# Splitting w_o beside the last group of products, and putting a chunk's state and the next chunk's turning side by side in a Mamba-2 and pooling step

## The chip, the cores and the metric

The kernel runs on one core of a Trainium2 chip. A core has a matrix engine (TensorE, "PE" in the profile, with its weight loads as "PEld"), a vector engine (VectorE, "DVE"), a scalar engine (ScalarE, "ACT"), a general engine (GpSimd, "POOL") and a queue engine (SyncE, "SP") that only issues DMAs. The metric is the device time of one execution in microseconds (us), as the median of several runs. Line numbers (L1213 and so on) are those of the kernel before.

## The reference, cut to what matters

One layer is computed for 1024 prompt positions and 64 sample positions (T = 1088 in all) with a model width of 1024:

```python
proj = h @ w_in                                   # u_pool, z_pool, z_ssm, xBC, dt, g
p = (pool_mix(u_pool) * silu(z_pool)) @ w_pool_out
# SSD over chunks of 128 positions, 4 groups of 8 heads, for every chunk in turn:
acs   = cumsum(dq * A);  decay = exp(acs_i - acs_j) under the causal mask
att   = (Cq Bq^T) * decay * dq
y     = att @ xq + (Cq * exp(acs)) @ h            # within the chunk, and from the state
h     = h * exp(last) + Bq^T ((exp(last - acs) * dq) * xq)
y     = rmsnorm((y + D * x) * silu(z_ssm)) ;  s = y @ w_ssm_out
x     = x + gate * ((sigmoid(g_pool) * p + sigmoid(g_ssm) * s) @ w_o)
```

All is float32. The large products are done as three passes of a shorter format (fp32r): a matrix is split into a high part (a rounded copy) and a low part (the difference), and hi·hi, hi·lo and lo·hi are added up in PSUM. A split therefore takes one copy on ACT and one subtraction on POOL or DVE.

## The kernel before

**Stages.** Up to 818 us of the profiled execution the kernel normalises the input, makes the projection with `w_in` and handles the sample positions. Then comes the **chunk stage**, which the change reorders: 32 chunks of the prompt (4 groups of heads, `g`, times 8 chunks of 128 positions, `c`), run one after the other. The change calls one of these a row of the sequence, and the prediction does so too. Beside the rows run the **products**: 8 units of `w_pool_out` (P_unit, L1711) and 24 units of `w_ssm_out` for the first three groups (S_unit, L1727), each in three pieces of 12 matmuls (L359 to L361), 96 pieces in all. After them comes the **last group of products**, S_unit for group 3 with the merging of the branches (tail_unit, L1907), and then the **output rows**, the product with `w_o` (from L1978).

**A row** is the generator `chunk` (L1488), cut by `yield` into steps that the loop at L1798 calls by hand:

1. loads (L1490 to L1494) of x, B and C (`xb`) and of the decay exponents (`dec`), 3 buffers each;
2. exponentials: ACT makes `cE` (L1498), POOL masks `dec` (L1192), ACT takes 8 exponentials (L1201);
3. **turning** (L1502 to L1525): PE transposes x and B (L1506, L1508) and multiplies B with C (L1509) into the PSUM tiles `px` and `pbc`; ACT copies `bt` (L1511) and C into `pbc` (L1513); DVE makes `xd` (L1517), `xw` (L1519), `dec` times CB (L1520) and `cE` times C (L1522); ACT makes `xD` (L1525);
4. **state and sums** (L1527 to L1543): PE makes the update `pu` (L1530, needs `bt` and `xw`) and the 16 products of `inner` (L1213 with `xd` and `dec`, L1216 with the state and `cE`); POOL scales the state (L1536), DVE adds `pu` (L1538); DVE adds the sums (`v`, L1542) and `finish` gates and squares them (L1468 to L1479);
5. for the last chunk of a group, the final state is turned and stored (L1546 to L1551).

**What sets the order.** All matmuls that are traced between two calls of `in_line` (L1792 and L1822) are chained, so PE does them exactly as the loop traces them. On ACT, DVE, POOL and SP a scheduler orders instructions by trace order among those that its own timeline has ready; each engine then works strictly in that order. `products(t)` (L1785) makes pieces until 2.56 times `t` have been made, so a row gets two or three. `behind(engine, n)` queues the instructions of a block behind the n-th last one traced on that engine; rows 1 and 2 are turned behind DVE (L1802). PSUM has three buffers for products (PA), four for px, pbc and the sums (PB) and one for `pu` (PC). Before the loop, 4 pieces (FRONT) are made and row 0 is turned.

**w_o before.** `wo_splits` (L1766) reads `w_o` in 16 halves of 256 KB (`pw`, two buffers), copies the high part on ACT (`ph`, L1777, one buffer), stores it from ACT's queue (L1778), subtracts on POOL (L1779) and stores the low part from SP (L1773), all to DRAM (`wo_d`). It is called from the thirteenth row of the loop on. In the last group of products, `wo_prep(k)` (L1859) loads both parts back. `m_split` (L1868) splits the merged branch, and `samples[m]` multiplies its sample positions (L1877).

Of the kernel before, what the change touches and what calls it, by code (L numbers as in the profile page):

```python
# [8 lines left out]
F32 = mybir.dt.float32  # L9
F32R = mybir.dt.float32r  # L10
AF = mybir.ActivationFunctionType
ALU = mybir.AluOpType
# [8 lines left out]
P = 128  # L21
D = 1024
# [24 lines left out]
def tile_pool_ssd_step(  # L47
# [6 lines left out]
    nc = tc.nc  # L54
    uid = [0]

    def nm(s):
        uid[0] += 1
        return f"{s}_{uid[0]}"
# [10 lines left out]
    def open_(name, bufs, side="left"):  # L70
        cm = tc.tile_pool(name=name, bufs=bufs, side=side, reuse_waits="tile")
        kept.append(cm)
        return cm.__enter__()
# [36 lines left out]
    load = nc.sync.dma_start  # L110
    store_ = nc.scalar.dma_start
    mm = nc.tensor.matmul
    act = nc.scalar.activation
    V = nc.vector
# [275 lines left out]
    def dram(name, shape, dt=F32):  # L390
        return dr.tile(list(shape), dt, tag=name, name=name)
# [13 lines left out]
    def behind(engine, n=0):  # L405

        of = (i for i in reversed(nc.cur_bb.bb.instructions) if i.engine == engine)
        for _ in range(n):
            next(of)
        return tc.issue_after(next(of))  # L410
# [1280 lines left out]
    seq = []  # L1691
# [14 lines left out]
    ck = right.__enter__()  # L1706
# [48 lines left out]
    def pieces():  # L1755
        ws = first_ws
        nxt = len(ws)
        for i, (pf, run) in enumerate(prods):
            while nxt < len(prods) and nxt <= i + 1:
                ws[nxt] = prods[nxt][0]()  # L1760
                nxt += 1
            yield from run(ws.pop(i))
    pc_ = pieces()
    wo_d = [dram(f"wo{k}", [P, 2, D]) for k in range(8)]

    def wo_splits():  # L1766
        raws = {}
        for n in range(18):
            if n < 16:
                raws[n] = ck.tile([P, 512], F32, tag="pw", name=nm("pw"), bufs=2)  # L1770
                load(raws[n], w_o[0, n // 2 * P:n // 2 * P + P, n % 2 * 512:n % 2 * 512 + 512])
            if n > 1:
                load(wo_d[(n - 2) // 2][:, 1, n % 2 * 512:n % 2 * 512 + 512], raws.pop(n - 2))  # L1773
            yield
            if n < 16:
                hi = ck.tile([P, 512], F32R, tag="ph", name=nm("ph"), bufs=1)
                act(hi, raws[n], AF.Copy)  # L1777
                store_(wo_d[n // 2][:, 0, n % 2 * 512:n % 2 * 512 + 512], hi.bitcast(F32))  # L1778
                nc.gpsimd.tensor_tensor(raws[n].bitcast(F32R), raws[n], hi.bitcast(F32), ALU.subtract)  # L1779
            yield  # L1780
    wos = wo_splits()
    RATE = 2.56
    FRONT = 4

    def products(t):  # L1785

        nonlocal made
        while made < RATE * t:
            next(pc_, None)
            made += 1  # L1790
# [5 lines left out]
        next(pc_)  # L1796
    next(seq[0])
    for i in range(len(seq)):  # L1798
        if i > 12:
            next(wos, None)  # L1800
        if i + 1 < len(seq):
            with behind(mybir.EngineType.DVE, 1 - i) if i < 2 else ExitStack():  # L1802
                next(seq[i + 1])
        products(i + 0.4)
        if i > 0:
            next(seq[i - 1], None)
        if i > 12:
            next(wos, None)
        next(seq[i], None)
        if i % NC == 3:  # L1810
            sample_end(i // NC)
        if i + 3 < len(seq):
            next(seq[i + 3])
        if i + 2 < len(seq):
            with behind(mybir.EngineType.Activation) if i == 0 else ExitStack():
                next(seq[i + 2])
        products(i + 1.0)
    next(seq[-1], None)
    for it in (pc_, wos):
        for _ in it:  # L1820
            pass
    in_line((mybir.EngineType.PE,))  # L1822
    right.__exit__(None, None, None)
    while right_all:
# [3 lines left out]

    mp = ctx.enter_context(tc.tile_pool(name="mp", bufs=8, side="right", reuse_waits="tile"))
    mq = open_("mq", 5)  # L1830

    def M(shape=(P, T), dt=F32):
        return mq.tile(list(shape), dt, tag="m", name=nm("m"))
# [7 lines left out]
    for c in range(9):  # L1841
        n = min(P, T - c * P)
# [5 lines left out]
    for c in range(9):  # L1848
        n = min(P, T - c * P)
# [4 lines left out]
    wo, mh, ml = [None] * 8, [None] * 8, [None] * 8  # L1854
    w4 = [Y4(hp), Y4(hp)]
    pso = [PB(), PC()]
    samples = []

    def wo_prep(k, mem):  # L1859
        if k < 4:  # L1860
            hi, lo = w4[0][:, k, :D], w4[1][:, k, :D]
        else:
            hi, lo = mem((P, D), F32R), mem((P, D), F32R)
        load(hi.bitcast(F32), wo_d[k][:, 0])
        load(lo.bitcast(F32), wo_d[k][:, 1])
        wo[k] = (hi, lo)

    def m_split(k, mem):  # L1868

# [37 lines left out]
    def tail_unit(m):  # L1907
        pf, run_ = S_unit(3, m, m_done)

        def run(w):  # L1910
            for _ in run_(w):
                pass
            if m < 5:
                wo_prep(m, M)
            if m < 7:
                m_split(m, M8 if m < 4 else G)
            if m < 5:
                with tc.high_priority(PRIO):
                    samples[m]()
        return (pf, run)  # L1920
    run_units([tail_unit(m) for m in range(8)])
    y4 = [Y4(hs), Y4(hs)]
# [4 lines left out]
    for k in (5, 6):  # L1927
        wo_prep(k, late)
        samples[k]()
# [119 lines left out]
```

## Time and profile before

| | us |
|---|---|
| median of 3 runs (1295.9 to 1298.21) | 1296.04 |
| the profiled execution, its own time | 1297.28 |
| its span, first to last instruction | 1295.4 |
| up to the first product beside the rows | 818.5 |
| opening, to the first product after row 0 | 18.8 |
| rows 1 to 31 with their products | 275.7 |
| rest of the products, last group of products | 83.8 |
| output rows, end | 98.6 |

The mean granted clock of TensorE is 0.996. In the profile's timeline a row gives start, duration, engine, line, operation, output and inputs, count, and in brackets how long the engine sat idle before it and what ended that. Matmuls overlap: the distance from one start to the next is the time one takes, and the duration (0.32 us for a distance of 0.16) is longer. A row "x4" merges four neighbours.

### The profile page before, as it was taken

The numbers are of one execution on the slowest core, as the hardware profiler recorded it, in microseconds if no ns is written. First come the engines' busy times: TensorE is split into PE (matmuls) and PEld (weight loads), VectorE is DVE, ScalarE is ACT, GpSimd is POOL, SyncE is SP. The second block draws the span as 40 slices with busy tenths as digits, with TensorE's granted clock in tenths as the row PEclk, the third lists the DMA queues.
The fourth block names the chain that finished last, engine by engine and source line by source line (L and its number), as shares of the span: only waits on it lengthen the run. The fifth ranks groups of instructions, "written<-read, shape, count | busy, mean of one in ns | idle before, by whom it ended". The sixth has DMA issues, their size and how long they took to land.

```text
span 1295.4 us, 26382 instructions
## 1 busy us (share of the span) xinstructions
PE 1258.9 (97%) x9739; PEld 1170.7 (90%) x9739; DVE 893.3 (69%) x1512; ACT 699.5 (54%) x1658; POOL 671.9 (52%) x563
## 2 busy tenths in 40 slices
PE   7999999999999999999999999999998999999998
PEld 6779999989999999999999999888897889999786
DVE  4686678966979688676766675577665877476433
ACT  4665347365656555555666543687886776201111
POOL 1007668677868777564445444266675656214000
PEclk9999999999999999999999999999999999999999
DMA  9736355465456544444566574999887665475631
GB/s 330 242 115 223 113 163 164 147 203 177 136 161 212 157 144 149 151 146 135 169 182 192 154 207 159 336 362 382 296 270 249 200 210 171 160 262 161 227 105 50
DMA packets 233793, 251.68 MB, mean 194 GB/s; under 512 B 31265, under 2 KB 177905, under 8 KB 233658
## 3 DMA queue, kind: packets, MB, share of 16 engines
q1 hardware_dynamic: 161568, 171.60, 41.6%
q10 hardware_dynamic: 72098, 78.41, 17.6%
q8 instruction: 77, 1.26, 0.4%
q14 instruction: 50, 0.41, 0.1%
HBM read 167.06 MB, written 83.01 MB: 193 GB/s over the span
## 4 chain that ended last, share of the span: by engine, by line
PE 73%; issue 8%; DMA 6%; POOL 4%; ACT 4%; DVE 4%; ACTq 0%; SPq 0%; POOLq 0%; DVEq 0%
PE mm L608 7%; PE ps L608 7%; PE ps L609 7%; PE ps L610 7%; PE mm L610 6%; PE mm L609 6%; PE mm L359 4%; PE mm L360 4%; PE mm L361 4%; PE ps L1213 2%; PE ps L1997 2%; PE ps L1995 2%; PE ps L1996 2%; PE pc L1530 2%; PE ps L1216 2%
## 5 line engine op out<-in xcount | busy, mean ns | idle before, releaser
L168 POOL TENSOR_TENSOR wlo<-rawA,whi 128x512 fp32r<-128x512 f32 x120 | 180.0, 1505 | 176.8 <-ACT whi L165 100.3
L168 POOL TENSOR_TENSOR wlo<-raw,whi 128x512 fp32r<-128x512 f32 x92 | 147.2, 1607 | 123.2 <-ACT whi L165 109.3
L359 PE MATMUL mm<-Y,whi 128*128 128x352 f32 (+1 forms) x480 | 164.2, 342 | 2.0 <-ACT G L1739 1.4
L360 PE MATMUL mm<-Y,whi 128*128 128x352 f32 (+1 forms) x480 | 158.1, 329 | 1.0 <-DVE Y L1566 1.0
L361 PE MATMUL mm<-Y,wlo 128*128 128x352 f32 (+1 forms) x480 | 157.5, 328 | 0.0
L608 PE MATMUL mm<-Y,whi 128*128 128x272 f32 x496 | 146.5, 295 | 0.7 <-DVE GA L624 0.5
L610 PE MATMUL mm<-Y,wlo 128*128 128x272 f32 x496 | 144.2, 291 | 2.9 <-POOL wlo L168 2.4
L608 PE MATMUL ps<-Y,whi 128*128 128x272 f32 x496 | 143.4, 289 | 2.3 <-ACT o L808 2.2
L609 PE MATMUL ps<-Y,whi 128*128 128x272 f32 x496 | 143.0, 288 | 0.0
L609 PE MATMUL mm<-Y,whi 128*128 128x272 f32 x496 | 142.6, 288 | 0.0
L610 PE MATMUL ps<-Y,wlo 128*128 128x272 f32 x496 | 142.6, 287 | 0.0
L1056 DVE SCALAR_TENSOR_TENSOR GA<-GA,cvT,GA 128x1112 f32<-128x1112 f32 x72 | 128.5, 1787 | 1.6 <-ACT GA L1053 1.5
L165 ACT ACTIVATE whi<-rawA 128x512 fp32r<-128x512 f32 x125 | 78.3, 627 | 88.8 <-PE ps L609 44.9
L165 ACT ACTIVATE whi<-raw 128x512 fp32r<-128x512 f32 x96 | 58.9, 627 | 105.7 <-DVE raw L554 51.3
L359 PEld LDWEIGHTS mm<-Y,whi 128*128 128x128 f32 x480 | 90.8, 189 | 8.8 <-issue 4.6
L610 PEld LDWEIGHTS mm<-Y,wlo 128*128 128x128 f32 x496 | 93.4, 188 | 4.7 <-POOL wlo L168 3.5
L608 PEld LDWEIGHTS mm<-Y,whi 128*128 128x128 f32 x496 | 93.3, 188 | 3.4 <-ACT whi L165 0.7
L608 PEld LDWEIGHTS ps<-Y,whi 128*128 128x128 f32 x496 | 93.3, 188 | 2.9 <-ACT o L808 2.4
L609 PEld LDWEIGHTS mm<-Y,whi 128*128 128x128 f32 x496 | 93.4, 188 | 0.9
L610 PEld LDWEIGHTS ps<-Y,wlo 128*128 128x128 f32 x496 | 93.4, 188 | 0.0
L609 PEld LDWEIGHTS ps<-Y,whi 128*128 128x128 f32 x496 | 93.3, 188 | 0.0
L360 PEld LDWEIGHTS mm<-Y,whi 128*128 128x128 f32 x480 | 90.8, 189 | 1.7 <-DVE Y L1566 1.6
(450 smaller groups left out, 3801.1 us busy)
## 6 DMA issues: line engine op xcount, KB each, us to landing
rawA<-in_w_in SPq DMA_DIRECT2D x46, 512.0 KB
dec<-acs_d SPq DMA_DIRECT2D x32, 512.0 KB
xbc<-GA ACTq DMA_DIRECT2D x24, 512.0 KB
xb<-xbc SPq DMA_DIRECT2D x32, 384.0 KB
rawA<-in_w_in SPq DMA_DIRECT2D x32, 256.0 KB
pw<-in_w_ssm_out ACTq DMA_DIRECT2D x32, 256.0 KB
ws<-ph ACTq DMA_DIRECT2D x32, 256.0 KB
ws<-pw SPq DMA_DIRECT2D x32, 256.0 KB
```

Source lines behind the costliest of these rows:

```text
L165: ins = act(hi[:, :, :ncols], raw[:, :, :ncols], AF.Copy)
L168: (eng or nc.gpsimd).tensor_tensor(lo[:, :, :ncols], raw[:, :, :ncols], hi[:, :, :ncols].bitcast(F32), ALU.subtract)
L359: mm(ps[:, :n], a, rh[k][:, o:o + n], start=(k == 0), stop=False)
L360: mm(ps[:, :n], a, rl[k][:, o:o + n], start=False, stop=False)
L361: mm(ps[:, :n], b, rh[k][:, o:o + n], start=False, stop=(k == nk - 1))
L608: mm(p, hi, ah, start=(k == 0), stop=False)
L609: mm(p, hi, al, start=False, stop=False)
L610: mm(p, lo, ah, start=False, stop=(k == 3))
L1056: V.scalar_tensor_tensor(d[:, :n], rp[:, k:k + n], cvT[:, 24 * k + mc:24 * k + mc + 1], d[:, :n], ALU.mult, ALU.add)
L1213: mm(o[hh], xd[:S, 2 * q + hh, :], dec[:S, 2 * q + hh], start=True, stop=state is None)
L1216: mm(o[hh], state[:, h * 64:h * 64 + 64], cE[:, h], start=False, stop=True)
L1530: mm(pu, bt, xw.rearrange("p h d -> p (h d)"), start=True, stop=True)
```

## The change

In the loop, the products between a row's turning and the next state go, and the order is turned round: row i's state and sums come first, right behind them row i+1 is turned, and then all the products of the row follow in one block. `wo_splits` goes from the loop. Instead `wo_prep` splits the first five slices of `w_o` (k < LATE = 5) in SBUF beside the last group of products, from raw slices of 512 KB; for the last three, `wo_store` splits them there too (low part on DVE), stores them in DRAM from SP, and `wo_prep` loads them back as before. `samples[m]` is called one unit later. A new pool `mr` holds two raw slices and one high part.

```diff
@@ the loop over the rows (-1796, +1781) @@
-        if i > 12:
-            next(wos, None)
+        if i > 0:
+            next(seq[i - 1], None)
+        next(seq[i], None)
         if i + 1 < len(seq):
             with behind(mybir.EngineType.DVE, 1 - i) if i < 2 else ExitStack():
                 next(seq[i + 1])
-        products(i + 0.4)
-        if i > 0:
-            next(seq[i - 1], None)
-        if i > 12:
-            next(wos, None)
-        next(seq[i], None)
         if i % NC == 3:
             sample_end(i // NC)
...
         products(i + 1.0)
@@ wo_prep (-1861, +1841) @@
-        load(hi.bitcast(F32), wo_d[k][:, 0])
-        load(lo.bitcast(F32), wo_d[k][:, 1])
+        if k < LATE:
+            raw = mr.tile([P, D], F32, tag="wr", name=nm("wr"))
+            load(raw, w_o[0, k * P:k * P + P, :])
+            act(hi, raw, AF.Copy)
+            nc.gpsimd.tensor_tensor(lo, raw, hi.bitcast(F32), ALU.subtract)
+        else:
+            load(hi.bitcast(F32), wo_d[k][:, 0])
+            load(lo.bitcast(F32), wo_d[k][:, 1])
...
+    def wo_store(k):
+        raw = mr.tile([P, D], F32, tag="wr", name=nm("wr"))
+        load(raw, w_o[0, k * P:k * P + P, :])
+        hi = mr.tile([P, D], F32R, tag="wh", name=nm("wh"), bufs=1)
+        act(hi, raw, AF.Copy)
+        load(wo_d[k][:, 0], hi.bitcast(F32))
+        V.tensor_tensor(raw.bitcast(F32R), raw, hi.bitcast(F32), ALU.subtract)
+        load(wo_d[k][:, 1], raw)
@@ tail_unit (-1910, +1905) @@
-            if m < 5:
+            if m < LATE:
                 wo_prep(m, M)
             if m < 7:
                 m_split(m, M8 if m < 4 else G)
-            if m < 5:
+            if 1 < m < 5:
+                wo_store(m + 3)
+            if 0 < m <= LATE:
                 with tc.high_priority(PRIO):
-                    samples[m]()
+                    samples[m - 1]()
```

More of the change, by code (lines that the diff above doesn't have):

```diff
@@ L1763, in tile_pool_ssd_step @@
     pc_ = pieces()
[L1764 to L1781, printed above, removed]
+    LATE = 5
+    wo_d = {k: dram(f"wo{k}", [P, 2, D]) for k in range(LATE, 8)}
     RATE = 2.56
@@ L1818, in tile_pool_ssd_step @@
     next(seq[-1], None)
-    for it in (pc_, wos):
-        for _ in it:
-            pass
+    for _ in pc_:
+        pass
     in_line((mybir.EngineType.PE,))
@@ L1830, in tile_pool_ssd_step @@
     mq = open_("mq", 5)
+    mr = open_("mr", 2)
     def M(shape=(P, T), dt=F32):
```

## The prediction, made before the change was run

> **What bounds the kernel now.** I read the page's busy shares first, then the engines' busy time by stage.
>
> ```profile
> PE 1258.9 (97%) x9739; PEld 1170.7 (90%) x9739; DVE 893.3 (69%) x1512; ACT 699.5 (54%) x1658; POOL 671.9 (52%) x563
> ```
> ```profile
> 837.30:1113.00 275.70, 270.51 (x2179) 240.03 (x2178) 198.77 (x269) 202.68 (x562) 177.96 (x205) 1.00 0.79 259
> 1113.00:1196.80 83.80, 83.21 (x492) 80.78 (x493) 50.51 (x89) 10.63 (x18) 23.92 (x13) 0.98 0.63 218
> ```
>
> PE is the bound in both stages the change touches: it is idle 5.2 of 275.7 us in the rows, 0.6 of 83.8 us in the last group. The change takes no matmul away. So it can win only seams between matmuls of different kinds and the little idle time, and it can lose wherever PE now has to wait. The second step was therefore PE's timeline, start by start, around one row (from 910 us), and at the first and last row with sums from the state.
>
> ```profile
> 910.38 0.60 PE L1506 MATMUL ps<-ident,xb 128*128 128x128 f32 x4
> ...
> 911.07 0.41 PE L359 MATMUL mm<-Y,whi 128*128 128x352 f32 x1
> 911.32 0.33 PE L360 MATMUL mm<-Y,whi 128*128 128x352 f32 x1
> 911.48 0.32 PE L361 MATMUL mm<-Y,wlo 128*128 128x352 f32 x1
> ...
> 913.09 1.02 PE L1530 MATMUL pc<-xw,bt 128*128 128x512 f32 x2
> 914.03 0.44 PE L1213 MATMUL ps<-dec,xd 128*64 128x128 f32 x4
> ...
> 915.93 0.43 PE L359 MATMUL mm<-Y,whi 128*128 128x352 f32 x1
> ```
> ```profile
> 845.04 0.43 PE L359 MATMUL mm<-Y,whi 128*128 128x352 f32 x1
> 845.30 0.32 PE L360 MATMUL mm<-Y,whi 128*128 128x352 f32 x1
> ...
> 1103.99 0.43 PE L359 MATMUL mm<-Y,whi 128*128 128x352 f32 x1
> 1104.26 0.32 PE L360 MATMUL mm<-Y,whi 128*128 128x352 f32 x1
> 1104.42 0.32 PE L361 MATMUL mm<-Y,wlo 128*128 128x352 f32 x1
> ```
>
> Turning takes 911.07 - 910.38 = 0.69 us, a piece of 12 matmuls 913.09 - 911.07 = 2.02, state and sums 915.93 - 913.09 = 2.84. A product matmul in full flow is 0.16 apart from the next; the first one behind small matmuls is 0.25 to 0.27 apart. So each return to the products costs some 0.1 us.
>
> **The change, part by part.**
>
> *Seams.* Before, a row returns to the products twice (behind turning, behind the sums); after, once. The one that goes costs 0.26 - 0.16 = 0.10 at the first row and 0.27 - 0.16 = 0.11 at the last; there are 31 of them. 31 x 0.105 = **-3.3 us**. Sums directly followed by transposes are nowhere in this trace: at worst that seam costs the same 0.11 (gain 0), at best the other return's 0.09 goes too (-6.0). I take -3.3, since both neighbours are then plain float32 matmuls, as the turning of rows 0 and 1 back to back was.
>
> *w_o out of the rows.* All the waits of PE recorded in rows 1 to 31 stand in one place:
>
> ```profile
> 978.86 0.43 PE L359 MATMUL mm<-Y,whi 128*128 128x352 f32 x1 [1.42 <-ACT G L1739]
> ...
> 980.74 0.32 PE L361 MATMUL mm<-Y,wlo 128*128 128x352 f32 x1
> 983.15 0.63 PE L1506 MATMUL ps<-ident,xb 128*128 128x128 f32 x4 [2.09 <-DVE cE L1522]
> ```
> ```profile
> 1002.84 0.30 PE L1508 MATMUL ps<-ident,xb 128*128 128x128 f32 x1 [1.68 <-DVE cE L1522]
> ```
> ```profile
> 975.61 0.63 ACT L1777 ACTIVATE ph<-pw 128x512 fp32r<-128x512 f32 x1 [2.96 <-DMA pw<-in_w_o]
> ...
> 991.97 0.63 ACT L1777 ACTIVATE ph<-pw 128x512 fp32r<-128x512 f32 x1 [4.82 <-DMA wo<-ph]
> ```
>
> The eviction (L1739) that PE waited for at 978.86 is queued on ACT behind the w_o copy that waited 2.96 us for its load. The copies of C that release `dec` and `cE` on DVE are queued behind the same copy and, before 1002.84, behind the one that waited 4.82 us for its buffer's store. Without w_o in the stage these waits go: 1.42 + (983.15 - 980.74 - 0.16 = 2.25) + 1.68 = 5.35, **-5.4 us**. Late next would be DVE itself, in the row estimate below; if half came back, the gain would be 2.7.
>
> *The opening.* Here the products taken out from between were cover. PE's, ACT's and DVE's timelines:
>
> ```profile
> 828.53 0.39 PE L1509 MATMUL ps<-xb 128*128 128x128 f32 x2
> ...
> 834.79 1.12 PE L1530 MATMUL pc<-xw,bt 128*128 128x512 f32 x2 [1.26 <-ACT bt L1511]
> 836.29 1.09 PE L1213 MATMUL ps<-dec,xd 128*64 128x128 f32 x16 [0.37 <-DVE dec L1520]
> 837.31 0.44 PE L359 MATMUL mm<-Y,whi 128*128 128x384 f32 x1
> ```
> ```profile
> 832.44 2.14 ACT L1201 ACTIVATE dec<-dec,acT 128x128 f32<-128x128 f32 x7
> 834.49 0.25 ACT L1511 ACTIVATE bt<-ps 128x128 f32<-128x128 f32 x1
> ```
>
> Row 0 is turned by 828.8, but its `bt` stands on ACT behind row 1's exponentials, till 834.74 (the trace order of all this stays). In that gap PE now turns row 1 and makes two pieces (0.69 + 2 x 2.0 = 4.7 us). After, state 0 follows turning 0 at once: PE is idle from 828.8 to 834.8. Of what follows it saves the stretch of state 0 (837.31 - 834.79 = 2.52, against 914.03 - 913.09 = 0.94 and 837.31 - 836.29 = 1.02 with its inputs ready: 0.56), since row 1's `xd` no longer stands ahead of `dec` on DVE. 4.7 - 0.6 = **+4.1 us**. If the scheduler put `bt` first, state 0 could start near 830 and nothing would be lost: bounds 0 and +4.7.
>
> *The clock.* A wait of 6 us is longer than any that PE has beside the rows, and the trace shows what a lull can do:
>
> ```profile
> 1135.02 2.05 PE L1843 MATMUL ps<-ones,sq_acc 128*128 128x1 f32 x18
> ```
> ```profile
> 1138.40:1141.80 3.40, 3.40 (x13) 3.40 (x12) 0.68 (x2) 0.00 (x0) 0.00 (x0) 0.52 0.98 374
> ```
>
> After 2 us of one-column matmuls PE runs 3.4 us at a granted clock of 0.52: 3.4 x 0.48 = 1.6 us lost. The wait of 2.09 us at 983.15 cost nothing of the kind. I take **+1.6 us** for the opening (bounds 0 and twice that, 3.2). The Trainium skill ("TensorE: Matmul & The Clock Gate", section "HAM oscillation — how this bites in real kernels") warns of gaps over about 3.4 us, after which PE restarts at half rate; it speaks against this change, and an estimate from its window, 3.4 us at half rate, is 1.7 us. This trace differs in that a lull with PE recorded as busy was enough.
>
> *Inside the rows.* Turning and the next state had a whole row and a piece between them; now they have the row's two or three pieces (82 pieces over 32 rows: 18 rows with three, 14 with two). What DVE, ACT and POOL have to do:
>
> ```profile
> L1520 DVE TENSOR_TENSOR dec<-dec,ps 128x1024 f32<-128x1024 f32 x30 | 36.6, 1218 | 29.1 <-ACT ps L1513 10.8 <-POOL sz L1475 7.3 <-issue 2.6
> L1522 DVE TENSOR_TENSOR cE<-cE,ps 128x1024 f32<-128x1024 f32 x27 | 32.8, 1214 | 0.0
> L1468 DVE TENSOR_TENSOR v<-v,sz 128x512 f32<-128x512 f32 x32 | 29.7, 930 | 0.6
> L1542 DVE TENSOR_TENSOR v<-ps,xD 128x512 f32<-128x512 f32 x32 | 22.0, 686 | 5.1 <-PE ps L1216 4.7 <-PE ps L1213 0.4
> L1519 DVE TENSOR_TENSOR xw<-ps,wdT 128x512 f32<-128x512 f32 x30 | 20.6, 686 | 19.9 <-PE pc L1530 19.9
> L1517 DVE TENSOR_TENSOR xd<-ps,dtT 128x512 f32<-128x512 f32 x30 | 20.5, 682 | 3.2 <-PE ps L1506 3.2
> ...
> L1742 DVE TENSOR_TENSOR G<-mm,G 128x352 f32<-128x352 f32 x24 | 12.3, 518 | 5.4 <-PE mm L361 5.4
> ```
> ```profile
> L1498 ACT ACTIVATE cE<-dec 128x1024 f32<-128x1024 f32 x27 | 28.4, 1051 | 15.5 <-PE ps L1216 9.5 <-DMA dec<-acs_d 5.4 <-DMA wlo<-ws 0.6
> ```
> ```profile
> L1192 POOL TENSOR_SCALAR_AFFINE_SELECT dec<-dec 128x1024 f32<-128x1024 f32 x30 | 34.9, 1165 | 13.4 <-DVE dec L1520 4.5 <-DMA dec<-acs_d 3.3 <-ACT cE L1498 3.0
> ```
>
> From the end of the sums DVE owes, in trace order, v 0.69, v·sz 0.93, xd 0.68, xw 0.69, dec 1.22, cE 1.21 = 5.42 us. PE needs `dec` after 0.69 + 2 x 2.0 + 0.94 = 5.6 us in a two-piece row, 7.6 in a three-piece row. The state's sum (L1538) fits into the 1.9 us of the inner products. So it just fits: I take **0**. If one eviction (0.52) slips in between, the two-piece rows are 0.34 late: 14 x 0.34 = +4.8. If ACT does the next row's cE and exponentials before this row's `bt` and C copy, these come after 1.05 + mask 1.17 + 2.45 (2.14 x 8/7) = 4.7 us, and dec and cE end at 7.1, 1.5 late: 14 x 1.5 = +21. Against it: those exponentials are traced later, and with sums first, `xD`'s buffer is free early, which ACT waited for before. Below nothing it can't go, as no other wait is left there.
>
> *The last group of products.* Added: a POOL subtraction of 128x1024 for five units, a DVE one for three, eight ACT copies; SP stores six slices of 512 KB. The nearest row:
>
> ```profile
> L1779 POOL TENSOR_TENSOR pw<-pw,ph 128x512 fp32r<-128x512 f32 x16 | 21.0, 1312 | 12.9 <-ACT ph L1777 12.9
> ```
>
> POOL: 5 x 2 x 1.31 = 13.1 us on top of 23.9 of 83.8. ACT: 8 x 2 x 0.63 = 10.1 on 10.6. DVE: 3 x 1.22 = 3.7 on 50.5. DMA: eight raw loads and six stores, 7 MB, for ten loads, 5 MB: 24 GB/s on 218. All have room; PE's matmuls hide it. But DVE's subtraction waits for a load and a copy, with the evictions queued behind; SP's low store waits for DVE, with the next unit's weights and gates behind it. Such a copy waited up to 4.82 us; PE's other two product buffers cover two pieces, 4.0: at most 3 x 0.8 = 2.4, doubled for the merged rows that the output needs, +5. Lighter loads at its start could give 1 back. I take **+0.5**.
>
> Sum: -3.3 - 5.4 + 4.1 + 1.6 + 0 + 0.5 = **-2.5 us**, on the profiled execution's 1297.28 (span 1295.4 and 1.9 around it): 1294.8. That execution lies 1.24 above the median of 1296.04; the sum holds for the median alike: **1293.5**.
>
> **The rivals.** (1) *The two-piece rows wait for DVE and ACT* (slower). For it: 0.2 us of room, and DVE's wait of 10.8 us for C copies in the row above. Against it: some of that came from w_o. Between +4.8 and +21, say +12: 1296.04 - 2.5 + 12 = 1305.5. It decides the sign from 14 x 0.2 us on. (2) *The last group gives the gain back*: +5 instead of +0.5: 1298.0. (3) *The opening costs nothing*, because `bt` goes ahead: -5.7: 1287.8. Against it: nothing ahead of turning 0 changes. (4) *The clock gives way in each row*: state and turning now make 2.84 + 0.69 = 3.5 us of small matmuls in a row, and L1843's 2 us were enough once. 31 x 1.6 = +50: 1343. Against it: 2.84 us never did in 31 rows. The same page ("Part 4: PE-mode transpose") says that transposes don't count as busy for the clock; by that rule this rival would hold; no run here shows it yet.
>
> **How the numbers follow.** Forecast 0.55, with its own range of 1289 to 1298 (best seam and half the opening; one eviction per short row); rivals 0.25, 0.10, 0.07, 0.03. A measurement of this kernel can tell about 0.2%, 2.6 us, from no change. The forecast sits on that bound: 0.30 faster, 0.22 same, 0.03 slower. With rival 3 faster is 0.37; rival 1 gives slower 0.22 and same 0.03, rival 2 gives 0.07 and 0.03, rival 4 0.03: same 0.28, slower 0.35. The range leaves out rival 4 and the far ends of 1 and 3: 1287 to 1308.
>
> **What would show it.** Right: turning starts where the sums end; no L1739 or cE wait around a row with w_o; PE idle some 6 us before row 0's `pu`, on `bt`, then about 3.4 us at half clock; DVE's cE ends before the next state's L1216. Wrong: waits of L1213, L1216 or L1530 on `dec`, `cE` or `xw` in two-piece rows (rival 1), waits of L359 on weights or L1898 in the last group (2), a clock below 1 in the rows' windows (4).

## The result and the profile after

The changed kernel takes **1304.09 us** (median of 6 runs, 1303.29 to 1306.42), the kernel before in the same comparison 1295.97 (6 runs, 1292.31 to 1298.21). The ratio is 1.0069, with a 95% interval of 1.0053 to 1.0086: slower by 7 to 11 us, where 1293.5 had been forecast. The time lies inside the range of 1287 to 1308. The profiled execution of after took 1303.29 us (span 1301.5), 6.0 more than that of before (1297.28).

Line numbers up to L1760 are those of before. Further down they are five less in the functions that the prediction names: L1872 is the samples' product (L1877 before), L1893 and L1898 are the eviction and the merge (L1898 and L1903), L1867 is the samples' subtraction (L1872), L1883 the load of a `gs` gate (L1888). In the new code, L1847 and L1848 are the copy and the subtraction of `wo_prep`, L1858 and L1860 those of `wo_store`.

Page line first, then engines by stage: the rows after the opening, and the rest up to where the output rows are in full flow.

```profile
PE 1258.7 (97%) x9739; PEld 1170.6 (90%) x9739; DVE 902.4 (69%) x1515; ACT 697.9 (54%) x1650; POOL 661.7 (51%) x552
```
```profile
839.17:1117.10 277.93, 274.23 (x2203) 244.47 (x2203) 199.71 (x272) 191.76 (x545) 153.80 (x188) 0.99 0.68 210
1117.10:1203.50 86.40, 81.09 (x488) 78.15 (x487) 62.31 (x92) 18.65 (x27) 36.67 (x18) 1.00 0.69 233
```

TensorE does the same work in the same busy time (1258.7 against 1258.9). So the 6 us are idle time. To find its places I cut TensorE's timeline into turnings, states with sums, and pieces of products, and took each one's distance to the next. By that reckoning:

| stage, from one start to the next | before | after | difference |
|---|---|---|---|
| up to the first product | 818.5 | 817.8 | -0.8 |
| first product to the last group's final state (L1548) | 296.4 | 301.2 | +4.8 |
| products that are left | 20.1 | 20.1 | 0 |
| last group, up to the first output row | 53.3 | 56.2 | +2.9 |
| output rows | 100.3 | 99.8 | -0.6 |

**The opening.** TensorE's timeline, then ScalarE's:

```profile
827.24 0.60 PE L1506 MATMUL ps<-ident,xb 128*128 128x128 f32 x4
...
833.89 2.08 PE L1530 MATMUL pc<-xw,bt 128*128 128x512 f32 x2 [5.72 <-ACT bt L1511]
...
835.89 1.98 PE L1213 MATMUL ps<-dec,xd 128*64 128x128 f32 x16
...
837.80 1.12 PE L1506 MATMUL ps<-ident,xb 128*128 128x128 f32 x4
```
```profile
831.54 2.14 ACT L1201 ACTIVATE dec<-dec,acT 128x128 f32<-128x128 f32 x7
833.58 0.26 ACT L1511 ACTIVATE bt<-ps 128x128 f32<-128x128 f32 x1
```

As forecast, `bt` stands behind row 1's exponentials and TensorE waits 5.72 us. State 0 then takes 3.91 us (833.89 to 837.80) and the turning behind it 1.37 (to 839.17), about twice what they take in later rows (1.98 without sums from the state, and 0.75). The clock, and the clock of the undisturbed rows:

```profile
833.00:838.00 5.00, 4.11 (x19) 2.28 (x20) 1.70 (x3) 4.60 (x14) 0.81 (x1) 0.50 0.44 132
925.00:1117.00 192.00, 192.00 (x1558) 171.47 (x1558) 140.60 (x191) 136.91 (x389) 112.17 (x141) 1.00 0.61 182
```

The half clock (0.50) costs 1.93 + 0.62 = 2.6 us. Against before, the opening loses 6.6 us: 4.5 in the gap, 1.4 in the state (3.91 against 2.52), 0.7 in the turning.

**The seams.** An undisturbed row:

```profile
1016.72 1.02 PE L1530 MATMUL pc<-xw,bt 128*128 128x512 f32 x2
...
1019.57 0.66 PE L1506 MATMUL ps<-ident,xb 128*128 128x128 f32 x4
...
1020.32 0.41 PE L359 MATMUL mm<-Y,whi 128*128 128x352 f32 x1
1020.56 0.32 PE L360 MATMUL mm<-Y,whi 128*128 128x352 f32 x1
```

State and sums take 2.85 us as before, and the one return to the products costs 0.09. But the turning, 1020.32 - 1019.57 = 0.75, took 0.69 before. Over the whole stage 65 returns at 0.10 became 34 at 0.09, -3.5 us, and 31 turnings cost 0.057 more each, +1.8: together about -1.6.

**One row.** From 925 us on no row waits at all. The waits of before at 978.86, 983.15 and 1002.84 are gone. But the second row of the second group of heads waits three times:

```profile
916.47 1.12 PE L1530 MATMUL pc<-xw,bt 128*128 128x512 f32 x2 [0.67 <-ACT bt L1511]
...
919.93 0.44 PE L1213 MATMUL ps<-dec,xd 128*64 128x128 f32 x4 [2.34 <-DVE dec L1520]
...
921.06 0.70 PE L1216 MATMUL ps<-cE,hst 128*64 128x128 f32 x4 [0.69 <-DVE cE L1522]
```

The waits make 3.7 us. Around them the clock gave way, here in the window behind the second one:

```profile
919.90:925.00 5.10, 4.38 (x38) 3.81 (x39) 2.34 (x3) 1.50 (x4) 2.78 (x5) 0.67 0.86 277
```

At 0.67 that window costs another 5.1 x 0.33 = 1.7 us. By the distances the row loses 5.8 in all, as much as the w_o waits had cost. The rows of SP's queue, then ScalarE's:

```profile
891.42 0.32 SPq L1883 DMA_DIRECT2D R<-gs  x1
...
892.48 0.56 SPq L1187 DMA_DIRECT2D dec<-acs_d  x1
...
904.00 0.53 SPq L1503 DMA_DIRECT2D sz<-z  x1
904.64 0.56 SPq L1187 DMA_DIRECT2D dec<-acs_d  x1
```
```profile
898.93 1.06 ACT L1498 ACTIVATE cE<-dec 128x1024 f32<-128x1024 f32 x1 [4.44 <-DMA dec<-acs_d]
899.90 0.61 ACT L1469 ACTIVATE sz<-v 128x512 f32<-128x512 f32 x1
...
909.84 1.06 ACT L1498 ACTIVATE cE<-dec 128x1024 f32<-128x1024 f32 x1 [4.99 <-DMA dec<-acs_d]
```

Read in order of time, a chain goes round twice. A gate load for the last group (`R<-gs`), placed here by the scheduler 250 us ahead of its use, waits on SP for an earlier tile's store (4.5 us by SP's waits), with the next decays' load queued behind it. ScalarE waits 4.44 us for those decays. So its gating of the row before (899.90) is late, and GpSimd's sums behind that too (L1473, till 903.97). The buffer for the next `z` load comes free late, that load goes out at 904.00, and the decays behind it at 904.64. ScalarE waits 4.99 us again, and `bt`, `dec` and `cE` are late for TensorE.

**The last group.** TensorE, VectorE, GpSimd, and the group of the samples' subtractions:

```profile
1167.12 0.50 PE L1872 MATMUL ps<-Y,sh 128*128 128x512 f32 x1 [2.19 <-DVE sh L1867]
...
1172.49 0.44 PE L359 MATMUL mm<-Y,whi 128*128 128x384 f32 x1 [1.54 <-DVE G L1893]
```
```profile
1162.62 2.02 DVE L1860 TENSOR_TENSOR wr<-wr,wh 128x1024 fp32r<-128x1024 f32 x1 [2.56 <-ACT wh L1858]
1164.56 2.51 DVE L1867 TENSOR_TENSOR sh<-G,sh 128x64 fp32r<-128x64 f32 x1
```
```profile
1157.89 3.16 POOL L1848 TENSOR_TENSOR Y<-wr,Y 128x1024 fp32r<-128x1024 f32 x1 [8.08 <-DMA wo<-wr]
1161.01 5.97 POOL L1899 TENSOR_TENSOR G<-G,m 128x1088 f32<-128x1088 f32 x2
```
```profile
L1867 DVE TENSOR_TENSOR sh<-G,sh 128x64 fp32r<-128x64 f32 x5 | 6.9, 1389 | 0.0
```

Three things are to be seen. VectorE waits 2.56 us for ScalarE's copy, as the prediction feared. And a subtraction of 128x64, which takes 0.21 us where it is alone (1177.90 in the same trace), takes 2.51 and ends at 1167.07, right after GpSimd's passes end (1166.98). These two passes are merging adds, which before has too, but here they stand right behind a subtraction of `wo_prep` (L1848). For that one GpSimd had been idle for 8.08 us: ScalarE's copy of the same slice (1156.75) had waited 5.47 us for its load (the store that the bracket names landed just as that copy ended). The stage is 2.9 us longer, or 4.5 if one leaves out that before lost 1.6 us here to its clock (the 0.52 shown with the prediction) and after did not.

### The profile page after: what moved, and what is told of

Same layout as the page of the kernel before. It is cut to its first block, busy times and chain, and to the rows that moved or that the text cites. A ratio compares the mean times of both kernels' runs of the same rounds, so it can differ in the third digit from the quotient of the medians.

```text
span 1301.5 us, 26330 instructions
## 1 busy us (share of the span) xinstructions
PE 1258.7 (97%) x9739; PEld 1170.6 (90%) x9739; DVE 902.4 (69%) x1515; ACT 697.9 (54%) x1650; POOL 661.7 (51%) x552
## 4 chain that ended last, share of the span: by engine, by line
PE 78%; DMA 6%; issue 5%; DVE 5%; ACT 3%; POOL 2%; SPq 1%; ACTq 0%; POOLq 0%; DVEq 0%
PE ps L608 7%; PE ps L609 7%; PE mm L608 7%; PE ps L610 7%; PE mm L610 7%; PE mm L609 7%; PE mm L359 4%; PE mm L360 4%; PE mm L361 4%; PE ps L1213 3%; PE ps L1992 2%; PE ps L1994 2%; PE ps L1993 2%; PE pc L1530 2%; PE ps L1216 2%
## 5 line engine op out<-in xcount | busy, mean ns | idle before, releaser
L359 PE MATMUL mm<-Y,whi 128*128 128x352 f32 (+1 forms) x480 | 160.1, 333 | 2.7 <-DVE G L1893 2.7
L360 PE MATMUL mm<-Y,whi 128*128 128x352 f32 (+1 forms) x480 | 157.4, 328 | 1.0 <-DVE Y L1566 1.0
```

The lines of the kernel that those rows point to most:

```text
L359: mm(ps[:, :n], a, rh[k][:, o:o + n], start=(k == 0), stop=False)
L360: mm(ps[:, :n], a, rl[k][:, o:o + n], start=False, stop=False)
```

## The experiments

**The theories.** *A*: four separate costs and gains, as above (opening, one row, last group, against seams and w_o's waits). *B*: the closer rows wait for VectorE and ScalarE in general (the first rival). *C*: all of the loss is w_o in the last group (the second rival). Where the expectations speak of the first sample's end they mean the place where the first group of heads ends, and with the ninth row the one at 916 us.

| kernel | median, us | ratio to before, 95% interval | first product to L1548 | last group and output rows |
|---|---|---|---|---|
| before (in the profile) | 1295.97 | 1 | 296.4 | 153.6 |
| after | 1304.09 | 1.0053 to 1.0086 | 301.2 | 155.9 |
| e1_order | 1309.48 | 1.0097 to 1.0135 | 310.8 | 151.6 |
| e2_wo | 1301.69 | 1.0034 to 1.0071 | 300.4 | 156.3 |
| e3_open | 1300.98 | 1.0029 to 1.0065 | 300.2 | 154.8 |
| e4_gs | 1300.23 | 1.0025 to 1.0056 | 299.0 | 156.6 |
| e5_tail | 1302.21 | 1.0034 to 1.0072 | 299.9 | 155.9 |
| e6_fill | 1301.72 | 1.0032 to 1.0067 | 300.7 | 154.9 |
| e7_old | 1300.84 | 1.0021 to 1.0050 | 298.6 | 157.8 |
| e9_mix | 1296.78 | 0.9995 to 1.0022 | 294.2 | 156.7 |
| e10_fo | 1296.02 | 0.9991 to 1.0023 | 297.3 | 156.7 |
| e11_oldfo | 1294.50 | 0.9982 to 1.0005 | 291.6 | 157.0 |
| e12_gap | 1293.54 | 0.9973 to 0.9996 | 290.8 | 156.5 |
| e13_gapold | 1293.81 | 0.9969 to 0.9994 | 294.0 | 155.1 |
| e14_dve | 1301.33 | 1.0029 to 1.0061 | 300.6 | 153.4 |
| e15_gapdve | 1291.91 | 0.9960 to 0.9985 | 291.5 | 154.3 |
| e16_gapnew | 1290.93 | 0.9947 to 0.9976 | 292.5 | 154.3 |

The last two columns come from one profiled execution each. Single waits in them move by a few us from one kernel to the next, so the medians decide. The last column also holds stretches of half clock, 1.7 us each, that have little to do with the edit: behind the one-column matmuls at the start of the last group in before, e2_wo, e7_old, e11_oldfo, e12_gap and e15_gapdve, and not in the others (last section).

### Each half of the change alone

The order alone (e1_order, w_o split within the rows as before):

```diff
 for i in range(len(seq)):
     if i > 12:
         next(wos, None)
+    if i > 0:
+        next(seq[i - 1], None)
+    next(seq[i], None)
...
-    products(i + 0.4)
-    if i > 0:
-        next(seq[i - 1], None)
     if i > 12:
         next(wos, None)
-    next(seq[i], None)
```

> The new order of the rows alone; w_o is still split within the rows as before. Theory A (four separate terms: the opening +6.6 us, one row of the profile after that waits 5.8 us for decay loads held up on SP's queue behind an early gs load, the seams -1.4, the last group's vector work +2 to +3.7, the w_o waits of the rows -5.4): here the opening and the seams are left, w_o's waits stay, and the SP queue may or may not hold a row: 1296.0 + 6.6 - 1.4 = 1301.2, up to 1307 if one row waits as in the kernel after. Theory B (two-piece rows wait on VectorE and ScalarE in general, rival 1 of the prediction): 1308 or more, with waits of TensorE in many rows. Theory C (all of the loss is w_o in the last group): 1296 or a little less.

It came out 2 us above the upper end of A, at B's 1308 or more. Many rows wait here, at 878, 897, 918, 948, 968 and 981 us. The heaviest after 925:

```profile
967.55 1.13 PE L1530 MATMUL pc<-xw,bt 128*128 128x512 f32 x2 [1.44 <-ACT bt L1511]
...
969.89 0.44 PE L1213 MATMUL ps<-dec,xd 128*64 128x128 f32 x4 [1.22 <-DVE dec L1520]
...
971.12 0.69 PE L1216 MATMUL ps<-cE,hst 128*64 128x128 f32 x4 [0.79 <-DVE cE L1522]
```

So rival 1 holds for closer rows *with* w_o's copies among them (in this trace ScalarE makes them from 839 us on, as the scheduler takes them ahead of their place in the loop): with w_o still there, the new order has no slack. In the kernel after, from 925 us on, the slack is enough. C falls: without any w_o in the last group the order alone is slower than the whole change.

w_o moved alone (e2_wo, old order):

```diff
-    if i > 0:
-        next(seq[i - 1], None)
-    next(seq[i], None)
...
+    products(i + 0.4)
+    if i > 0:
+        next(seq[i - 1], None)
+    next(seq[i], None)
```

> w_o beside the last group as in the kernel after; the rows in their old order, with products between the row's sums and the next row's turning and again before its state. Theory A: no opening loss, the w_o waits gone (-5.4), the last group +2 to +3.7: 1292.6 to 1294.3, unless the SP queue holds a row here as well (then 1298 to 1300). Theory B: about the same, 1291 to 1294. Theory C (all of the loss is w_o in the last group): 1304.

It came out at 1301.69, above A's bracket. The waits at 975 to 1003 are gone, but this kernel too loses 6 us in the row at 919 and 2 in the two before it. So neither half of the change is a gain by itself, and a row is lost at this place in the old order too. Its wait is another one, though. ScalarE's row:

```profile
919.68 1.28 ACT L1525 ACTIVATE xD<-xb,Dv 128x128 f32<-128x128 f32 x4 [4.93 <-DMA out<-xD]
```

ScalarE stands here for a store, not for decays; e7_old, below, takes that up.

### The opening

e3_open keeps the old order in the first row only:

```diff
-    next(seq[i], None)
+    if i > 0:
+        next(seq[i], None)
...
+    if i == 0:
+        products(0.4)
+        next(seq[0], None)
```

> The kernel after, but its first row keeps the old order: the next row's turning and a piece of products stand between the first row's turning and its state. Theory A: the wait of 5.72 us on the exponentials' transpose and the half-speed state behind it go, 1304.1 - 6.6 = 1297.5 (between 1297.5 and 1299 if a part of the wait comes back as stalls); the row held by the SP queue and the last group stay as they are. Theory C: 1304. If the opening only moves time that the exponentials' chain needs anyway: 1302 to 1304, with the wait showing up in the rows that follow.

1300.98: half of the 6.6 us came back. The wait on `bt` is 0.48 us and the state takes 3.18, but row 2 now loses 4.3 us to its decays, which ScalarE and GpSimd take up only behind row 1's skip terms (these wait 2.81 us for a buffer) and gating.

e6_fill puts idle products into the gap:

```diff
+    if i == 0:
+        fill = PB()
+        for n in range(34):
+            mm(fill[:, :352], ph_[0][:, 0:P], ph_[1][:, 0:352], start=True, stop=True)
     next(seq[i], None)
```

> The kernel after, with 34 products of 352 columns whose result nobody reads between the first row's turning and its state: they fill TensorE's wait of 5.7 us and lengthen nothing. If the state of 3.91 us and the turning of 1.37 behind that wait were slow because TensorE had stood idle (clock): they take 2.0 and 0.75 again, 2.6 us less, 1301.5. If they were slow for another reason (the operands' arrival, the order on other engines): 1304, the two pieces as long as before.

```profile
832.21 1.13 PE L1530 MATMUL pc<-xw,bt 128*128 128x512 f32 x2
...
841.29 1.02 PE L1530 MATMUL pc<-xw,bt 128*128 128x512 f32 x2
...
843.10 0.44 PE L1213 MATMUL ps<-dec,xd 128*64 128x128 f32 x4 [0.79 <-DVE dec L1520]
```

The state takes 2.34 us, the turning 0.74, and the granted clock of 832 to 837 us is 1.00. So the half speed came from the idle time before it. Row 1 comes sooner and now waits 1.7 us (L1530 to the end of its sums takes 4.52 instead of 2.85) for decays that were in time before: of 2.6 us that the clock cost, that row gives most back. From the first product to the end of row 1's sums it is 29.6 us against 30.3 in after. The median of 1301.72 agrees with the expected 1301.5, but the traces show only 0.65 us of that here.

### The row at 916 us

e4_gs puts the gate loads of the last group behind SP's earlier loads:

```diff
-        load(r, gs_d[m])
+        with behind(mybir.EngineType.SP):
+            load(r, gs_d[m])
```

> The kernel after, but the gs loads of the last group stand on SP's queue behind what was issued there before them in the program's order. Theory A: the ninth row's decay load is no longer held, its 5.8 us of waits go: 1298.3, the opening and the last group as in the kernel after; up to +2 if the gs loads then come late for the last group. Rival (the early gs load only happens to stand there, the row waits for the decays anyway, because ScalarE and the w_o-free rows run ahead of them): 1304, with the same waits of TensorE in that row.

```profile
917.62 0.44 PE L1213 MATMUL ps<-dec,xd 128*64 128x128 f32 x4 [1.12 <-DVE dec L1520]
918.75 0.44 PE L1216 MATMUL ps<-cE,hst 128*64 128x128 f32 x4 [0.69 <-DVE cE L1522]
```

1300.23, 3.9 us less. The row's loss falls from 5.8 to 2.1 us, and its decays' load goes out at 900.87 instead of 904.64. So the early gate load is the larger part of this row's loss, not all of it. What is left is ScalarE's wait of 1.56 us for a store; and another row, at 986, now loses 2.0 us to its decays. e7_old shows that second cause by itself: the old order, the same edit, and the three low halves of `wo_store` on GpSimd.

> w_o beside the last group as in the kernel after, the rows in their old order throughout (as e2_wo), with the early gs loads of the last group behind SP's earlier loads and the three low halves on GpSimd. Theory A: e2_wo's 1301.7 less its wait in the row after the first sample's end (6.4 us of its trace) less 1 to 4 in the last group: 1291 to 1294, under the kernel before at 1295.2. If the waits in that row come from somewhere else than the gs loads: 1298 to 1301.

It gave 1300.84, the case in which the gate loads are not the cause. ScalarE's and TensorE's rows:

```profile
910.06 0.40 ACTq L1551 DMA_DIRECT2D out<-xD  x1
...
916.97 1.27 ACT L1525 ACTIVATE xD<-xb,Dv 128x128 f32<-128x128 f32 x4 [4.97 <-DMA out<-xD]
```
```profile
921.68 0.45 PE L1508 MATMUL ps<-ident,xb 128*128 128x128 f32 x1 [4.61 <-DVE cE L1522]
```

Where a group of heads ends, the final state is stored from one of the two `xD` buffers, which are used for the skip terms. ScalarE comes to the next skip term at 912.00, 1.9 us after the store was issued, and stands 4.97 us until the store has landed. In before, other work (eight exponentials, evictions and a w_o copy) stood between, and `xD` came at 918.52, 8.8 us after the store was issued, without a wait. e11_oldfo gives the state a tile of its own:

```diff
-            fo = ckt([P, 4, P], "xD")
+            fo = ckt([P, 4, P], "fo", 1)
```

> As e7_old (old order of the rows, w_o in the last group), with the final state's store from a tile of its own. In e7_old's trace ScalarE stands 4.97 us in the row after the first sample's end until that store has landed, and TensorE loses 6.7 us there. If the store's tile is the cause: 1300.8 - 6.7 = 1294, a little under the kernel before; the forecast's gain of 5.4 by taking w_o out of the rows then shows, less the 4 us that the last group takes back. If something else holds that row (SP's loads of the decays): 1299 to 1301.

1294.50, as expected. Here the rows take 4.8 us less than before (291.6 against 296.4): the gain by taking w_o out of the rows, forecast at 5.4, is there once nothing else is late. The last group takes 3.4 back; TensorE waits there for one eviction for 3.09 us, with two stretches of half clock behind it.

### The order with these causes gone

e9_mix is e7_old with the new order from the fourth row on; e10_fo adds the tile for the state.

```diff
-    if i > 0:
+    if i > 2:
         next(seq[i - 1], None)
         next(seq[i], None)
...
+    if i < 3:
+        products(i + 0.4)
+        if i > 0:
+            next(seq[i - 1], None)
+        next(seq[i], None)
```

> As e7_old, but the new order from the fourth row on (the first three rows keep the old one, so the opening is that of before). Against e7_old this shows what the seams are worth alone: by the rows of the trace 29 x 0.05 = 1.5 us less (the prediction put 31 x 0.105 = 3.3), so 1289.5 to 1292.5 where e7_old gives 1291 to 1294. If rows that follow each other closely cannot have their decays in time at the samples' ends (4 us in the trace of e4_gs): 2 to 4 us more than e7_old.

> As e9_mix, but the final state of a sample is stored from a tile of its own and no longer from one of the two that the skip term uses. In e9_mix's trace ScalarE waits 1.24 us for that store in the row after the first sample's end, and TensorE loses 1.6 us there: 1295 to 1296.5 against e9_mix's 1296.8. If the row waits for its decays anyway: no difference.

e9_mix came out at 1296.78, 4 us over its bracket (which took e7_old at 1291 to 1294); e10_fo, at 1296.02, lies in its own, but 0.8 us is less than the two can tell. e9_mix is 4 under e7_old; by the traces that is e7_old's wait for the store, of which the closer rows keep 1.24 us. Against e11_oldfo, which lacks that wait too, e10_fo is 1.5 over, inside their scatter. Its trace, of an execution 3.2 us over its median, loses 5 us in one row, at 875. A load of a gate (`R<-gp`, L1718) had waited 6.2 us on SP, and behind it stood the loads of the group's sample positions (L1485, L1483), for whose gating ScalarE then stood 5.87 us. In e12_gap and e16_gapnew the same row loses 1.5 and 3.7 us. So the seams' gain is seen in the rows of a trace, but in no median: about as much is lost where a group of heads ends. That these losses are the whole difference is not shown.

### The last group

e5_tail: the kernel after, with `wo_store`'s subtraction on GpSimd.

```diff
-        V.tensor_tensor(raw.bitcast(F32R), raw, hi.bitcast(F32), ALU.subtract)
+        nc.gpsimd.tensor_tensor(raw.bitcast(F32R), raw, hi.bitcast(F32), ALU.subtract)
```

> The kernel after, but in the last group the low halves of the three stored blocks of w_o are subtracted on GpSimd instead of VectorE, so that VectorE no longer stands behind ScalarE's wait for the raw block there. If VectorE's place in that line is what made the products of the last group late (theory A, +3.7 in the tail against before): 2 to 4 us less, 1300 to 1302. If ScalarE's own wait for the raw blocks holds the samples' and the products' evictions anyway, or GpSimd's longer subtraction (2.4 against 1.2 us) makes its adds late in turn: 1303 to 1305.

1302.21, 1.9 us less, but the last group and the output rows take 155.9 us in both traces: what the profile gains (1301.5 to 1299.2) lies ahead of them, where the edit changes nothing. VectorE no longer stands behind ScalarE's copy. In its place, beside three more passes of GpSimd, its splits of the merged branch (L1878) take 2.41 us in the mean instead of 1.45, and TensorE waits 3.13 us in one place, with a stretch of half clock behind it. So the edit did nothing for its stage.

e12_gap (on e9_mix) and e13_gapold (on e7_old) take `wo_store` out of the last group and do the same work in six pieces of 128x512 (`ls`) beside the products that are left after the last row; the state is stored from one of these pieces' buffers.

```diff
-            if 1 < m < 5:
-                wo_store(m + 3)
...
-    for _ in pc_:
-        pass
+    for _ in pc_:
+        next(ls, None)
```

> As e9_mix (new order from the fourth row on), the final state's store from another tile, and the three blocks of w_o that go through DRAM are split in six pieces beside the products between the last row and the last group, where ScalarE stands idle for 19 us in the trace of the kernel after; the other five stay in the last group. If those three blocks' work is what the last group pays (4.4 us between e1_order and the kernel after): 1296.8 - 1 - 3 = 1291.5 to 1294. If the five that stay are the cause, or the six pieces end too late for the last group to begin: 1295 to 1299.

> As e12_gap with the old order of all rows, so the two differ by the seams and by what the closer rows wait. By e11_oldfo's expectation of 1294 less 3: 1290 to 1292 if both causes (the store's tile, the three blocks in the last group) are right, 1294 if only one of them is. e12_gap should be 1.5 under it by the seams, or 0 to 3 over it if the closer rows wait for their decays at the samples' ends.

1293.54, inside its bracket, and 1293.81, the value for one cause out of two. Without the half clock behind the one-column matmuls (1.7 us in e12_gap and in e7_old) the last group and the output rows are 1.9 us shorter than in e9_mix and 1.0 than in e7_old, still 3.2 and 3.5 over e1_order, so by these traces most of its loss lies with the five blocks that stay. Against e11_oldfo, which also stores the state from another tile, the median of e13_gapold is only 0.7 us less. In e13_gapold VectorE's rows show what the five do to it; VectorE, GpSimd, and the group:

```profile
1174.43 3.45 DVE L1896 TENSOR_TENSOR m<-G,m 128x1024 fp32r<-128x1024 f32 x1
```
```profile
1174.39 2.40 POOL L1866 TENSOR_TENSOR Y<-wr,Y 128x1024 fp32r<-128x1024 f32 x1
```
```profile
L1896 DVE TENSOR_TENSOR m<-G,m 128x1024 fp32r<-128x1024 f32 x4 | 11.0, 2742 | 0.0
```

A pass that takes 1.2 us alone takes 3.45: 2.36 until GpSimd's subtraction ends (1176.79), and then 1.09. Of the four, two more (3.14 and 3.16 us) stand beside merging adds, and one (1.21) beside nothing; in before, where GpSimd has no subtractions here, the four take 1.22 in the mean. e14_dve, e15_gapdve and e16_gapnew put `wo_prep`'s subtraction on VectorE in the kernel after, in e13_gapold and in e12_gap:

```diff
-            nc.gpsimd.tensor_tensor(lo, raw, hi.bitcast(F32), ALU.subtract)
+            V.tensor_tensor(lo, raw, hi.bitcast(F32), ALU.subtract)
```

> The kernel after, but the five low halves of w_o that stay in SBUF are subtracted on VectorE instead of GpSimd. In the trace of the kernel after, VectorE's short subtraction of the samples (L1867, 0.21 us alone) takes up to 2.51 us and ends with a pass of GpSimd. Theory P (a pass of GpSimd over two tiles in SBUF holds up a VectorE pass over two tiles in SBUF for its whole length, so GpSimd's five added passes of 2.4 us stretch VectorE's line): L1867 falls from a mean of 1.39 us towards the 0.63 of before, and the last group gets 1 to 3 us shorter although VectorE gets 5 x 1.22 = 6 us more work: 1301 to 1303. Theory Q (the waits for ScalarE and the raw blocks are all of it): 1304 to 1307, since VectorE only gets more work.

> As e13_gapold, with the five low halves on VectorE. There the passes of VectorE that split the merged branch take 2.74 us in the mean against 1.21 of before, each beside a pass of GpSimd. Theory P: they fall to 1.2 to 1.6 us, TensorE's waits in the last group (3.4 us in e13_gapold) to 1 to 2: 1291.5 to 1293 against 1293.8. Theory Q: 1294 to 1296.

> As e12_gap (new order from the fourth row on), with the five low halves on VectorE. Theory P: 1 to 2 less than e12_gap's 1293.5: 1291.5 to 1292.5, and within 1 us of e15_gapdve, as the closer rows give back by waits at the samples' ends what their seams save. If the seams are kept whole: 1.6 under e15_gapdve.

```profile
L1867 DVE TENSOR_TENSOR sh<-G,sh 128x64 fp32r<-128x64 f32 x5 | 5.1, 1020 | 0.0
```
```profile
L1900 DVE TENSOR_TENSOR m<-G,m 128x1024 fp32r<-128x1024 f32 x4 | 4.8, 1208 | 0.0
```

The first row is e14_dve's, the second e16_gapnew's. All three moved as theory P says: 2.8, 1.9 and 2.6 us less, although VectorE got 6 us more work; the 1.9 lie within the scatter of their executions (1288.1 to 1296.14 in e15_gapdve), the other two do not. In the kernel after, the last group and the output rows go from 155.9 to 153.4, and TensorE's waits in the last group from 5.3 to 2.9 us; in e13_gapold and e12_gap they go from 4.1 to 2.0 (e16_gapnew has one more at the start of the group, of 1.2 us). The samples' subtraction came down only to 1.02 us, not near 0.63: merging adds still stand beside it. The edit also takes 12 us off GpSimd, whose adds then come earlier (the first at 1158.38 instead of 1161.01), and it was not tried which of the two helps more. **e16_gapnew, at 1290.93, is faster than both kernels**, 0.39% under before (0.24 to 0.53%), and e15_gapdve, in the old order of the rows, 0.28% (0.15 to 0.40%). Between these two, which differ by the order alone, 1.0 us lies inside their scatter.

## Why the prediction was wrong, point by point

- **Seams** (forecast -3.3, measured -1.6): mechanism right, size off. The products gained 3.5. The step that failed is "Sums directly followed by transposes are nowhere in this trace", with the choice to let that seam cost nothing, on the ground that rows 0 and 1 were turned back to back. Such a turning costs 0.057 us more. The bound of 0 to -6.0 held it.
- **w_o out of the rows** (-5.4): right. The three waits are absent in after, e2_wo and e11_oldfo, and the rows of the last are 4.8 shorter. In the kernel after, the gain was eaten by the next point.
- **The opening** (+4.1): right. Without the clock it is 4.0 (6.6 less the clock's 2.6). e3_open and e6_fill add that only part of it can be had back, since the decays of rows 1 and 2 are next.
- **The clock** (+1.6, bounds 0 and 3.2): right in kind, 2.6 in size. The term took one stretch of 3.4 us; the half clock lasted twice that, with 5.25 us of it on work. e6_fill showed the cause.
- **Inside the rows** (taken as 0): this is a step that failed, by 5.8 us. It counted what VectorE, ScalarE and GpSimd owe between two states and left out SP's queue. The row at 916 waits for a load of decays that had stood behind other loads, and e4_gs recovered 3.9 us by moving one load. That "no other wait is left there" was no argument: what is late next was not an engine but a queue and a buffer. Rival 1, waits in two-piece rows from lack of room, did not come in the kernel after, but did in e1_order.
- **The last group** (+0.5): the second step that failed; +2.9, or +4.5 at an equal clock. The first half of rival 2, VectorE behind ScalarE's copy, is in the trace. The other half was in the sentence "All have room": 13.1 us were added to 23.9 on GpSimd, but not the time that each GpSimd pass takes from VectorE, nor the 8.08 us for which GpSimd stood for a late slice with the merging adds behind it. The Trainium skill ("SBUF — State Buffer", section "Who interferes with whom") says that a VectorE instruction with two inputs in SBUF contends with a GpSimd instruction that reads SBUF, and that the one that comes later waits for the other's end. The traces agree: 0.21 became 2.51 us beside a pass, and the evictions of 128x352, which have one of their inputs in PSUM, stayed at a mean of 0.51 in after and in e13_gapold.
- **Rival 3** fell, `bt` did not go ahead. **Rival 4** fell: 2.85 + 0.75 = 3.6 us of state and turning in each row, at a granted clock of 1.00 from 925 to 1117 us.

Summed from the traces: -0.8 before the first product, +6.6 opening, -1.6 seams, -5.8 w_o (with what stood around its waits), +5.8 the row at 916, +2.9 last group, -0.6 output rows. That is +6.5, against +6.0 between the two profiled executions and +8.1 between the medians (the profiled execution of before lies 1.3 over its median, that of after 0.8 under). Against the forecast of -2.5 the two largest misses are the row at 916, with 5.8, and the last group, with 2.4.

What stays open: why the scheduler's order brings out the early gate load's wait just there, in after, and not in before, where three such loads stood in the same stretch of SP's queue and none waited for a store; and whether the closer rows would keep their 1.6 us if those gate loads stood on another queue. Neither was tried.

## What to carry to other kernels

A row that is bounded by TensorE has more limits than its engines' busy time: list also each load that it needs, what stands ahead of it on its queue, and whose buffer that one waits for. Work that is taken out of a stage takes with it the delay that kept other things apart, such as a store and the next use of its buffer. Work that is moved to an idle engine is not free if its passes hold up a busy one; before moving it, look how long the busy engine's short passes take beside the idle engine's present ones.

## What the runs showed of the hardware beyond that

After 5.72 us of idle time TensorE ran at a granted clock of 0.50 for about 5 us, and at 1.00 where 34 products filled the gap. In e7_old a wait of 4.61 us was enough, and the piece of products behind it took 3.83 us instead of 2.0; the clock while it waited, and then behind the wait:

```profile
916.50:921.70 5.20, 0.59 (x6) 0.38 (x5) 2.52 (x3) 3.42 (x9) 0.00 (x0) 0.74 0.23 60
921.70:926.00 4.30, 4.30 (x15) 4.30 (x16) 3.33 (x5) 2.64 (x8) 3.13 (x3) 0.52 0.78 283
```

This wait cost its own length and 1.8 us more.

The traces show more than that. In all 17 the half clock comes in steps of 3.41 us, one or two at a time, and the steps of one execution begin whole multiples of 3.41 us apart (only the last one, at the end of the span, is cut off). Between 700 and 1200 us the traces have 2466 such steps at full clock. In 22 of them TensorE is idle for 1.95 us or more, in one piece or several, and all 22 are followed by a step at half clock. Of four with 1.79 to 1.90 us two are. Of the rest, with less, only six are, and these come below. Two steps of after, around the waits of 2.34 and 0.69 us:

```profile
917.65:921.06 3.41, 0.44 (x4) 0.20 (x5) 2.41 (x3) 3.11 (x9) 1.81 (x2) 1.00 0.94 349
921.06:924.48 3.42, 3.42 (x29) 3.09 (x30) 0.66 (x2) 0.12 (x1) 1.10 (x4) 0.50 0.85 259
```

In before, the wait of 2.09 us at 983.15 left 1.90 us in one step (981.25 to 984.67) and cost nothing.

The 18 one-column matmuls at the start of the last group, in which TensorE is recorded as busy, lowered the clock to 0.52 in before and to 0.54 in e2_wo and left it at 1.00 in after, with the same instructions ahead of them. Here too it is their place among the steps that decides: in the six traces in which the clock fell they begin 0.17 to 1.17 us after the start of a step, so that all 2.05 us lie inside it; in the eleven others they begin 1.62 to 3.20 us after it and run over into the next. So the time at which the group happens to begin moves a profile by some 1.7 us.
